# A conv and SwiGLU layer on one core: norm factors by Pool alone, ten of them through scratch, and another order at the end

## The chip, the cores and the metric

The kernel runs on one core of a Trainium2 chip. The core has five engines with instruction queues of their own, each worked off in order: TensorE (PE) multiplies matrices, VectorE (DVE), ScalarE (ACT) and GpSimd (POOL) work on tiles elementwise, SyncE (SP) issues DMAs. ACT issues DMAs too. The metric is the device time of one execution in microseconds (us).

## The reference, cut to what is computed

One layer runs over 2048 tokens of 1024 features in f32. The vector c gives six vectors (shift, scale and gate of two halves of the layer). The first half is a gated causal convolution of three taps, the second a SwiGLU FFN with 2816 hidden features. Each half has an RMS norm ahead of it and another behind it: four norms, each of which needs one factor per token.

```python
def rms_norm(x, g):
    xf = x.astype(jnp.float32)
    y = xf * lax.rsqrt(jnp.mean(xf * xf, axis=-1, keepdims=True) + RMS_EPS)
    return (y * g.astype(jnp.float32)).astype(x.dtype)
...
        mod = c_act @ ada_w[i] + ada_b[i]
        sh_m, sc_m, g_m, sh_f, sc_f, g_f = jnp.split(mod, N_ADA, axis=-1)
        h = modulate(rms_norm(x, norm_gains[i, 0]), sh_m, sc_m)
        h = short_conv_mixer(h, conv_w_in[j], conv_w[j], conv_w_out[j])
        x = x + g_m[:, None, :] * rms_norm(h, norm_gains[i, 1])
        h = modulate(rms_norm(x, norm_gains[i, 2]), sh_f, sc_f)
        h = swiglu(h, ffn_w_gate_up[i], ffn_w_down[i])
        x = x + g_f[:, None, :] * rms_norm(h, norm_gains[i, 3])
```

## The kernel before

**Tiles.** Features lie on the 128 partitions, tokens along the free axis. A tile is mostly 128x512: 128 features of one chunk of 512 tokens (CH). The 2048 tokens are two halves `u` = 0, 1, each of two chunks `tok` = 0, 1; 1024 features are 8 tiles (KD).

**Phases and slots.** The four matrix products of the layer (in, out, gu for gate and up, down) run once for each half, in the order in0, out0, in1, out1, gu0, down0, gu1, down1 (L864). Each is done with seven products P1 to P7 in place of eight, on sums of operands (A11, A12, A22, S1 to S4). Each operand is split into an upper and a lower part (names with h and l), so that a 128x128 by 128x512 product is three matmuls. A slot is four such products, twelve matmuls. A loop goes through the slots in order; weights are called up several slots ahead (`supply`: WHOLE 5, BLOCKS 9, SUMS 7, HIGH 5, LOW 4).

**Order.** Every operation goes through one helper (L78) that keeps it in the order in which it is written, on each engine; so all rows of the profile have line 78, and one goes by the names of tiles. The work beside the products is put between them by hand: `later(slots, f)` (L110) runs f so many slots on, and a generator that yields n goes on n slots later. A delay is a place in the order of the program, not a time.

**A norm factor.** Squares (ACT) are added up over feature tiles (POOL, for a part DVE), in a tile 128x512 such as `out0q`. `norm_of_sums` (L254) sums over the partitions on PE: four matmuls with `mean` as the moving operand leave the means of the squares as a 128x4 tile (token t*128 + p at partition p, column t); then `root` (L218) takes the power -0.5:

```python
        G.tensor_tensor(p, v, mhalf, ALU.pow)
        yield 1
        V.tensor_tensor(t, p, p, ALU.mult)
        V.tensor_tensor(t, t, v, ALU.mult)
        V.scalar_tensor_tensor(q, t, -3.0, p, ALU.add, ALU.mult)
```

The three DVE operations are a Newton step that gives -2 times the factor; so the gains in `vt` are scaled by -0.5 at the start (L158). As tokens lie along the free axis, the factor is then needed as a row, the same on all partitions: `diagonal` (L236) puts the 128x4 tile into four diagonal blocks (4 DVE operations), `spread` (L242) multiplies them by a matrix of ones (one f32 matmul, 128x512, into a PSUM bank) and ACT copies that to `rb`, of which there are two (NRB).

**Names.** r0 to r3 are the factors of the input norms, n00 to n11 (half, chunk) those of the norm behind out (`after_out`, L936), m00 to m11 those of the norm ahead of gu (spread as h00 to h11, L1381), o00, o01, o10 those of the norm behind down (`after_down`, L969), last that of the last chunk (`last_half`, L1011). A letter behind the name tells the step: s sums, v with EPS, p power, t and q the Newton step, d diagonal, b the spread in PSUM, r the copy.

**The end.** Behind the last matmul of down1, `last_half` sums the squares of the last chunk (`down1q`, seven tiles, and `lastq`, the eighth), makes the factor, spreads it (`lastb`), multiplies the eight tiles `down1z` with it on DVE and adds x: for tiles 4, 5, 6, 7, 0 (ON_PE) on PE, into PSUM banks `lastx` that hold x, with an ACT copy and a DMA of ACT behind; for tiles 1, 2, 3 on DVE, with a DMA of SP.

**The start.** `start` (L1076) computes c's vectors with DVE and PE (`ada`, `pms`, `mB`) and the first chunk's factor r0, while x and the first weights land. Matmuls on a constant tile (`warm`, L1203; tile `w`) keep PE busy meanwhile.

Of the kernel before, what the change touches and what calls it, by code (L numbers as in the profile page):

```python
# [10 lines left out]
F32 = mybir.dt.float32  # L11
# [38 lines left out]
def hybrid_conv_layer(  # L50
# [107 lines left out]
    V.tensor_scalar(vt[:, VG : VG + 4 * KD], vt[:, VG : VG + 4 * KD], -0.5, None, ALU.mult)  # L158
# [59 lines left out]
    def root(v, name):  # L218

        p, t = small(4, name + "p"), small(4, name + "t")  # L220
        G.tensor_tensor(p, v, mhalf, ALU.pow)
        yield 1
        q = sb.tile([P, 4], F32, tag="q", bufs=8, name=name + "q")
        V.tensor_tensor(t, p, p, ALU.mult)
        V.tensor_tensor(t, t, v, ALU.mult)
        V.scalar_tensor_tensor(q, t, -3.0, p, ALU.add, ALU.mult)
        return q
# [21 lines left out]
    def spread_later(q, name, put, lag=4):  # L249
        dg = diagonal(q, name)  # L250
        yield lag
        put(spread(dg, name))

# [260 lines left out]
    class Group:  # L514
# [134 lines left out]
        def ready_z(self, c):  # L649
            ph = self.ph  # L650
            tok, n = {"11": (0, self.i), "12": (0, self.i + 4), "21": (1, self.i), "22": (1, self.i + 4)}[c]
            z = ph.z(tok, n)
            if c == "12":
                A.copy(z, self.pa)
            ph.tiles_done[tok] += 1
            scaled_z = partial(A.activation, z, z, AF.Copy, scale=col(mG[1], n))
            if ph.last and ph.tiles_done[1] == KD:
                ph.sq = tmp("lastq")
                A.activation(ph.sq[:, :CH], z, AF.Square)
                scaled_z()  # L660
            else:
                add_square(ph.acc, tok, z, f"{ph.name}q{tok}{n}", V if ph.last and c == "21" else G, 0.5 if ph.last else 1)
                if ph.last and tok:
                    later(1, scaled_z)
            ph.tile_ready(tok, n, z)
            if ph.tiles_done[tok] == KD:
                ph.half_ready(tok)

    def add_square(acc, key, z, name, E=G, lag=1):
        if key not in acc:  # L670
            acc[key] = tmp(name)
            A.activation(acc[key][:, :CH], z, AF.Square)
        else:
            sq = tmp(name)
            A.activation(sq[:, :CH], z, AF.Square)
# [260 lines left out]
    def after_out(ph, tok):  # L936
# [5 lines left out]
        yield (24 if u == 0 else 34) + 8 * tok  # L942
        yield from spread_later(q, f"n{u}{tok}", partial(put, rb, 0))
# [23 lines left out]
        rb1[u, tok] = yield from norm_of_sums(acc[0], f"m{u}{tok}")  # L967

    def after_down(ph, tok):  # L969
# [8 lines left out]
        if not ph.last:  # L978
            yield 22 + 10 * tok
        yield from spread_later(q, f"o{u}{tok}", partial(put, rb, 0), 2 if ph.last else 4)  # L980
# [28 lines left out]
    ON_PE = (4, 5, 6, 7, 0)  # L1009

    def last_half(ph):  # L1011
# [8 lines left out]
        st = bank("lasts")  # L1020
        for k in ON_PE[:2]:
            add_x(k)
        for i, sq in enumerate((ph.acc[tok], ph.sq)):
            for t in range(4):
                PE.matmul(col(st, 4 * i + t), sq[:, t * P : (t + 1) * P], mean, start=True, stop=True)
        for k in ON_PE[2:]:
            add_x(k)
        v = small(4, "lastv")
        V.tensor_scalar(v, st[:, :4], EPS, None, ALU.add)
        V.tensor_tensor(v, v, st[:, 4:8], ALU.add)  # L1030
        dg = diagonal(at_once(root(v, "last")), "last")
        b = bank("lastb")
        PE.matmul(b, one, dg[:, :CH], start=True, stop=True)
        for k in ON_PE + tuple(k for k in range(KD) if k not in ON_PE):
# [6 lines left out]
            else:  # L1041
                V.tensor_tensor(xt, xt, z, ALU.add)
# [315 lines left out]
    for ph in phases[1:]:  # L1358
# [18 lines left out]
        else:  # L1377
            rb = {}
            src = lambda t, tok, kk, u=ph.u: SP.dma_start(t, x1_d[u][tok][:, kk * 4 : kk * 4 + 4, :])
            for tok, op in ((0, "P1"), (1, "P7")):  # L1380
                go = lambda u=ph.u, tok=tok, rb=rb: run(spread_later(rb1[u, tok], f"h{u}{tok}", partial(put, rb, tok)))  # L1381
                at(op, -14 - 2 * ph.u, go)
# [101 lines left out]
```

## Time and profile before

| | us |
|---|---|
| median of 3 runs | 1967.44 (1966.73 to 1967.9) |
| the profiled execution | 1968.11 |
| its span | 1966.3 |
| PE busy in the span | 1939.7 |
| DMA moved | 459.51 MB, mean 234 GB/s |
| granted PE clock, mean | 0.999 |

The span runs from the first to the last instruction of the trace; the profiled execution's own time is 1.8 us longer. Starts in the timeline count from the beginning of the span. "Busy" counts an engine's own operations, and matmuls are pipelined, so that two in a row overlap in the rows. A row of the timeline gives start, duration, engine, operation, out<-in, shape and, in brackets, the idle time of the engine ahead of it and who ended it.

The last matmul of down1 ends at 1946.5 us. The slices of the page show PE at nine tenths or more in all but the first and the last:

```profile
PE   8899999999999999999999999999999999999998
DMA  9369979769996764677665987477554342386534
```

### The profile page before, as it was taken

The page shows a single profiled execution, that of the slowest core. Times are in us where ns is not written, and L with a number is a line of the kernel's source. Part 1 is how long each engine was busy: PE and PEld are TensorE (multiplying, and loading weights), DVE is VectorE, ACT ScalarE, POOL GpSimd, SP SyncE. Part 2 cuts the span into 40 slices and gives each one's busy share as a digit, 9 for nine tenths or more (in the row PEclk, how much of TensorE's full clock was granted, in tenths as well). Part 3 has the DMA queues.
Part 4 walks back from the last instruction along what each step waited for, and adds up shares of the span by engine and source line. Part 5 has one row for each costly group of instructions (what it writes and reads, how often), then busy time and mean ns, then how long its engine had stood idle before and what let it go on. Part 6 is the DMA issues. An engine that isn't in the chain of part 4 may idle for free.

```text
span 1966.3 us, 24998 instructions
## 1 busy us (share of the span) xinstructions
PE 1939.7 (99%) x8468; PEld 1572.9 (80%) x8468; DVE 1463.6 (74%) x2159; ACT 870.3 (44%) x1430; POOL 343.1 (17%) x224
## 2 busy tenths in 40 slices
PE   8899999999999999999999999999999999999998
PEld 4578887878888888888888888888888888888886
DVE  5998898978998876997776765586776655665466
ACT  4633457534336643443333454463333333444452
POOL 0012112311221301244331310120100100111010
PEclk9999999999999999999999999999999999999999
DMA  9369979769996764677665987477554342386534
GB/s 389 137 230 378 332 248 352 267 214 362 324 315 236 263 222 148 223 241 248 208 216 186 304 297 261 183 278 267 199 192 135 125 142 97 118 316 229 197 132 133
DMA packets 204752, 459.51 MB, mean 234 GB/s; under 512 B 22864, under 2 KB 38352, under 8 KB 198224
## 3 DMA queue, kind: packets, MB, share of 16 engines
q1 hardware_dynamic: 180000, 403.52, 59.4%
q10 hardware_dynamic: 24624, 54.40, 7.2%
q8 instruction: 66, 1.08, 0.2%
q14 instruction: 62, 0.51, 0.1%
HBM read 326.75 MB, written 131.07 MB: 233 GB/s over the span
## 4 chain that ended last, share of the span: by engine, by line
PE 92%; DVE 3%; issue 2%; DMA 2%; ACT 1%; POOL 0%; ACTq 0%; POOLq 0%; SPq 0%; DVEq 0%
PE gu0P L78 21%; PE gu1P L78 21%; PE in0P L78 11%; PE down0P L78 11%; PE in1P L78 10%; PE down1P L78 9%; PE out1P L78 4%; PE out0P L78 3%; DMA x<-xx 0%; DMA in0a<-xt_d 0%; DMA c<-c_row_d 0%; PE pms L78 0%; DVE down1z L78 0%; DVE in1y L78 0%; DMA in7P2k<-kin7P 0%
## 5 line engine op out<-in xcount | busy, mean ns | idle before, releaser
L78 DVE TENSOR_TENSOR gu1a<-gu1P,gu1a 128x512 f32<-128x512 f32 x63 | 43.5, 691 | 108.7 <-PE gu1P L78 108.7
L78 DVE TENSOR_TENSOR gu0a<-gu0P,gu0a 128x512 f32<-128x512 f32 x63 | 43.3, 688 | 69.5 <-PE gu0P L78 67.7
L78 POOL TENSOR_TENSOR gu1a<-gu1a 128x512 f32<-128x512 f32 x11 | 19.0, 1726 | 363.5 <-DVE gu1g11s L78 42.5
L78 ACT COPY gu1a<-gu1P 128x512 f32<-128x512 f32 x42 | 24.7, 588 | 98.5 <-PE gu1P L78 87.4
L78 POOL TENSOR_TENSOR nq<-nq,nq 128x512 f32<-128x512 f32 x28 | 41.4, 1477 | 133.8 <-ACT nq L78 129.0
L78 ACT COPY gu0a<-gu0P 128x512 f32<-128x512 f32 x42 | 24.5, 588 | 84.3 <-PE gu0P L78 81.5
L78 DVE CUSTOM_DVE_ANT_0 ada<-ada,c 128x512 f32<-128x512 f32 x80 | 60.1, 761 | 0.0
L78 ACT COPY gu1g<-gu1P 128x512 f32<-128x512 f32 x24 | 14.1, 589 | 92.9 <-PE gu1P L78 92.9
L78 POOL TENSOR_TENSOR down0q<-down0q,down0q 128x512 f32<-128x512 f32 x14 | 23.9, 1706 | 144.1 <-ACT down0q L78 144.0
L78 POOL TENSOR_TENSOR gu0a<-gu0a 128x512 f32<-128x512 f32 x11 | 18.2, 1658 | 170.5 <-ACT gu0a L78 47.5
L78 ACT COPY gu0g<-gu0P 128x512 f32<-128x512 f32 x24 | 14.1, 589 | 75.9 <-PE gu0P L78 75.4
L78 POOL TENSOR_TENSOR down1q<-down1q,down1q 128x512 f32<-128x512 f32 x10 | 16.1, 1615 | 148.6 <-ACT down1q L78 148.5
L78 DVE TENSOR_TENSOR gu1g<-gu1P,gu1g 128x512 f32<-128x512 f32 x24 | 16.6, 691 | 27.4 <-ACT gu1g L78 26.0
L78 DVE TENSOR_TENSOR down2P<-down2P,down2P 128x512 fp32r<-128x512 f32 x14 | 12.0, 854 | 28.6 <-ACT down2P L78 28.6
L78 ACT ACTIVATE gu1a<-gu1a 128x512 f32<-128x512 f32 x42 | 26.6, 633 | 13.2 <-DVE xo L78 6.0
L78 ACT ACTIVATE gu0a<-gu0a 128x512 f32<-128x512 f32 x42 | 26.6, 632 | 11.5 <-DVE gu0a L78 10.2
L78 POOL TENSOR_TENSOR out1q<-out1q,out1q 128x512 f32<-128x512 f32 x14 | 22.3, 1594 | 51.3 <-ACT out1q L78 51.2
L78 POOL TENSOR_TENSOR out0q<-out0q,out0q 128x512 f32<-128x512 f32 x14 | 22.5, 1606 | 45.1 <-ACT out0q L78 44.9
L78 DVE TENSOR_TENSOR xx<-xx,zz 128x512 f32<-128x512 f32 x32 | 28.2, 880 | 1.1
L78 DVE TENSOR_TENSOR gu0g<-gu0P,gu0g 128x512 f32<-128x512 f32 x24 | 16.5, 689 | 14.7 <-ACT gu0g L78 13.3
L78 ACT ACTIVATE nq<-xx 128x512 f32<-128x512 f32 x32 | 20.2, 631 | 15.9 <-DVE xx L78 15.9
L78 DVE TENSOR_TENSOR down10P<-down10P,down10P 128x384 fp32r<-128x384 f32 x14 | 8.6, 615 | 22.0 <-ACT down10P L78 22.0
(3225 smaller groups left out, 6728.5 us busy)
## 6 DMA issues: line engine op xcount, KB each, us to landing
ada<-ada_d SPq DMA_DIRECT2D x64, 256.0 KB, 5.2
act0A<-gu0a SPq DMA_DIRECT2D x33, 256.0 KB, 3.5
act1A<-gu1a SPq DMA_DIRECT2D x33, 256.0 KB, 2.7
ada<-ada_d SPq DMA_DIRECT2D x16, 512.0 KB, 9.4
zz<-z SPq DMA_DIRECT2D x32, 256.0 KB, 5.5
xx<-xt_d SPq DMA_DIRECT2D x32, 256.0 KB, 5.4
x<-xx ACTq DMA_DIRECT2D x32, 256.0 KB, 5.5
down0S<-act0S SPq DMA_DIRECT2D x8, 1024.0 KB, 7.1
```

The lines of the kernel that those rows point to most:

```text
L78: return tc.keep_in_program_order(f(*args, **kwargs))
```

## The change

It has four parts.

1. `root` takes POOL's power as the factor. The three DVE operations behind it go in all norms, and the scaling of `vt` at the start with them (the factor is no longer -2 times itself).
2. Ten factors (n00, n01, n10, n11, those of m, and o00, o01) are no longer spread by a diagonal, PE and ACT. `keep_row` has ACT write the 128x4 tile, 16 bytes from each partition, into a row of 2 KB in DRAM eight slots after the factor is there; `repeat_later` has SP load that row to all 128 partitions (256 KB) eight slots ahead of its use. The point of use stays where it was. r0 to r3, o10 and last are spread as before.
3. So that 16 bytes of a partition are four tokens in a row, token p*4+t must end at partition p, column t. For that the 80 squares of the ten norms are written with their tokens in another order: ACT reads a tile in order and writes with a step of 128 elements (512 bytes). The squares of down1 stay as they are.
4. The end: the sums of the seven tiles of `down1q` stand on PE some slots ahead of the last products; the EPS is added to them; the diagonal and its spread go in four pieces, one after the other; two matmuls `lastw` fill PE behind them; tiles 4 to 7 are added on PE (and go out by ACT), 1 and 2 on POOL, 0 and 3 on DVE (and go out by SP), in the order 0, 4, 1, 5, 6, 2, 7, 3.

```diff
-    V.tensor_scalar(vt[:, VG : VG + 4 * KD], vt[:, VG : VG + 4 * KD], -0.5, None, ALU.mult)
...
     def root(v, name):
-        p, t = small(4, name + "p"), small(4, name + "t")
-        G.tensor_tensor(p, v, mhalf, ALU.pow)
+        q = sb.tile([P, 4], F32, tag="q", bufs=8, name=name + "q")
+        G.tensor_tensor(q, v, mhalf, ALU.pow)
         yield 1
-        q = sb.tile([P, 4], F32, tag="q", bufs=8, name=name + "q")
-        V.tensor_tensor(t, p, p, ALU.mult)
-        V.tensor_tensor(t, t, v, ALU.mult)
-        V.scalar_tensor_tensor(q, t, -3.0, p, ALU.add, ALU.mult)
         return q
...
+    def keep_row(q, name):
+        row = scratch([CH], name + "w")
+        later(8, lambda: A.dma_start(row.rearrange("(p t) -> p t", t=4), q))
+        return row
+
+    def repeat_later(row, name, put):
+        rb = sb.tile([P, CH], F32, tag="rb", bufs=NRB, name=name + "r")
+        SP.dma_start(rb, row.rearrange("(a n) -> a n", a=1).to_broadcast((P, CH)))
+        yield 8
+        put(rb)
...
-                add_square(ph.acc, tok, z, f"{ph.name}q{tok}{n}", V if ph.last and c == "21" else G, 0.5 if ph.last else 1)
+                add_square(ph.acc, tok, z, f"{ph.name}q{tok}{n}", V if ph.last and c == "21" else G, 0.5 if ph.last else 1, not ph.last)
                 if ph.last and tok:
                     later(1, scaled_z)
+                    if ph.tiles_done[1] == KD - 1:
+                        later(1.5, partial(all_but_one, ph))
...
-    def add_square(acc, key, z, name, E=G, lag=1):
+    def add_square(acc, key, z, name, E=G, lag=1, in_turn=True):
+        def square(t):
+            if in_turn:
+                A.activation(t[:, :CH].rearrange("p (t n) -> p n t", t=4), z.rearrange("p (n t) -> p n t", t=4), AF.Square)
+            else:
+                A.activation(t[:, :CH], z, AF.Square)
...
         q = yield from norm_of_sums(ph.acc[tok], f"n{u}{tok}")
-        yield (24 if u == 0 else 34) + 8 * tok
-        yield from spread_later(q, f"n{u}{tok}", partial(put, rb, 0))
+        row = keep_row(q, f"n{u}{tok}")
+        yield (20 if u == 0 else 30) + 8 * tok
+        yield from repeat_later(row, f"n{u}{tok}", partial(put, rb, 0))
...
-        rb1[u, tok] = yield from norm_of_sums(acc[0], f"m{u}{tok}")
+        q = yield from norm_of_sums(acc[0], f"m{u}{tok}")
+        rb1[u, tok] = keep_row(q, f"m{u}{tok}")
...
         q = yield from norm_of_sums(ph.acc[tok], f"o{u}{tok}")
-        if not ph.last:
-            yield 22 + 10 * tok
-        yield from spread_later(q, f"o{u}{tok}", partial(put, rb, 0), 2 if ph.last else 4)
+        if ph.last:
+            yield from spread_later(q, f"o{u}{tok}", partial(put, rb, 0), 2)
+        else:
+            row = keep_row(q, f"o{u}{tok}")
+            yield 18 + 10 * tok
+            yield from repeat_later(row, f"o{u}{tok}", partial(put, rb, 0))
...
-    ON_PE = (4, 5, 6, 7, 0)
+    ON_PE, ON_POOL, LAST_TURN = (4, 5, 6, 7), (1, 2), (0, 4, 1, 5, 6, 2, 7, 3)
+
+    def sums_of_squares(ph, sq, first):
+        for t in range(4):
+            PE.matmul(col(ph.st, t + 4 * first), sq[:, t * P : (t + 1) * P], mean, start=True, stop=True)
+
+    def all_but_one(ph):
+        ph.st = bank("lasts")
+        sums_of_squares(ph, ph.acc[1], True)
...
-        st = bank("lasts")
+        v = small(4, "lastv")
+        V.tensor_scalar(v, ph.st[:, 4:8], EPS, None, ALU.add)
         for k in ON_PE[:2]:
             add_x(k)
-        for i, sq in enumerate((ph.acc[tok], ph.sq)):
-            for t in range(4):
-                PE.matmul(col(st, 4 * i + t), sq[:, t * P : (t + 1) * P], mean, start=True, stop=True)
+        sums_of_squares(ph, ph.sq, False)
         for k in ON_PE[2:]:
             add_x(k)
-        v = small(4, "lastv")
-        V.tensor_scalar(v, st[:, :4], EPS, None, ALU.add)
-        V.tensor_tensor(v, v, st[:, 4:8], ALU.add)
-        dg = diagonal(at_once(root(v, "last")), "last")
-        b = bank("lastb")
-        PE.matmul(b, one, dg[:, :CH], start=True, stop=True)
-        for k in ON_PE + tuple(k for k in range(KD) if k not in ON_PE):
+        V.tensor_tensor(v, v, ph.st[:, :4], ALU.add)
+        q = at_once(root(v, "last"))
+        dg = tmp("lastd")
+        b, warm = bank("lastb"), bank("lastw")
+        for t in range(4):
+            c = slice(t * P, (t + 1) * P)
+            V.tensor_scalar(dg[:, c], ident, q[:, t : t + 1], None, ALU.mult)
+            PE.matmul(b[:, c], one, dg[:, c], start=True, stop=True)
+        for _ in range(2):
+            PE.matmul(warm, one, dg[:, :CH], start=True, stop=True)
+        for k in LAST_TURN:
...
-                V.tensor_tensor(xt, xt, z, ALU.add)
+                (G if k in ON_POOL else V).tensor_tensor(xt, xt, z, ALU.add)
...
-                go = lambda u=ph.u, tok=tok, rb=rb: run(spread_later(rb1[u, tok], f"h{u}{tok}", partial(put, rb, tok)))
-                at(op, -14 - 2 * ph.u, go)
+                go = lambda u=ph.u, tok=tok, rb=rb: run(repeat_later(rb1[u, tok], f"h{u}{tok}", partial(put, rb, tok)))
+                at(op, -18 - 2 * ph.u, go)
```

How this moves instructions, at three places of the program. First, PE's queue in gu1, where o00's factor is spread (`gu1P` are the PSUM banks of the products, behind the comma stands the operand that is loaded as weights). Before, and then of the change:

```order
L78 MATMUL gu1P_0_11326<-gu1S2h,gu0P6k 128x512 x2
L78 MATMUL gu1P_0_11326<-gu1S2l,gu0P6k 128x512
L78 MATMUL o00b<-o00d,one 128x512
L78 MATMUL gu1P_1_11347<-gu1S2h,gu1P6k 128x512 x2
L78 MATMUL gu1P_1_11347<-gu1S2l,gu1P6k 128x512
```
```order
L78 MATMUL gu1P_0_11222<-gu1S2h,gu0P6k 128x512 x2
L78 MATMUL gu1P_0_11222<-gu1S2l,gu0P6k 128x512
L78 MATMUL gu1P_1_11243<-gu1S2h,gu1P6k 128x512 x2
L78 MATMUL gu1P_1_11243<-gu1S2l,gu1P6k 128x512
L78 MATMUL gu1P_1_11243<-gu1S2h,gu1P6k 128x512 x2
```

The spread stood between two products and is gone; so it is at the nine other places. Second, ACT's queue in in1 where n00's factor is written, of the change (casts make the upper parts of operands, copies empty PSUM), and SP's queue where it is read (`gu0b` and `in6P` are weights, `kgu0P` and `y1A` stores):

```order
L78 ACTIVATE in1d<-in1d,mB_95 128x512 x4
L78 CAST in1S2h<-in1a 128x512 x4
L78 CAST in1S1h<-in1c 128x2048
L78 DMA n00w<-n00q 128x4
L78 CAST in1S4h<-in1b 128x2048
L78 COPY in1c_21_3431<-in1P_0_3230 128x512
```
```order
L78 DMA kgu0P_3595<-gu0P_3575 128x1024
L78 DMA kgu0P_3603<-gu0P_3597 128x1024
L78 DMA n00r<-n00w 128x512
L78 DMA in6P1k<-kin6P_1208 128x1024
L78 DMA y1A_106<-in1y_3552 128x512
```

Both DMAs are new and stand between rows that were neighbours before. Third, the end of PE's queue, before and then of the change (`down1P` is the last bank of the products, `xl` holds x):

```order
L78 MATMUL down1P_3_15723<-down1A_15793,down11P_16059 128x512
L78 MATMUL lastx_16146<-xl_15911,ident 128x512
L78 MATMUL lastx_16148<-xl_15913,ident 128x512
L78 MATMUL lasts<-mean,down1q_15853 128x1 x4
L78 MATMUL lasts<-mean,lastq 128x1 x4
L78 MATMUL lastx_16158<-xl_15915,ident 128x512
L78 MATMUL lastx_16160<-xl_15917,ident 128x512
L78 MATMUL lastx_16162<-xl_15903,ident 128x512
L78 MATMUL lastb<-lastd,one 128x512
L78 MATMUL lastx_16146<-down1z_15378,ident 128x512
```
```order
L78 MATMUL down1P_3_15602<-down1A_15667,down11P_15933 128x512
L78 MATMUL lastx_16026<-xl_15785,ident 128x512
L78 MATMUL lastx_16028<-xl_15787,ident 128x512
L78 MATMUL lasts<-mean,lastq 128x1 x4
L78 MATMUL lastx_16034<-xl_15789,ident 128x512
L78 MATMUL lastx_16036<-xl_15791,ident 128x512
L78 MATMUL lastb<-lastd,one 128x128 x4
L78 MATMUL lastw<-lastd,one 128x512 x2
L78 MATMUL lastx_16026<-down1z_15257,ident 128x512
```

The four sums of `down1q` are gone from here; they now stand 21 matmuls of `down1P` earlier, behind the products with `down3P`. The spread is four matmuls.

More of the change, by code (lines that the diff above doesn't have):

```diff
@@ L667, in ready_z @@
                 ph.half_ready(tok)
-    def add_square(acc, key, z, name, E=G, lag=1):
+    def add_square(acc, key, z, name, E=G, lag=1, in_turn=True):
[4 more added lines that the diff above has]
+                A.activation(t[:, :CH], z, AF.Square)
         if key not in acc:
             acc[key] = tmp(name)
-            A.activation(acc[key][:, :CH], z, AF.Square)
+            square(acc[key])
         else:
             sq = tmp(name)
-            A.activation(sq[:, :CH], z, AF.Square)
+            square(sq)
             later(lag, lambda: E.tensor_tensor(acc[key][:, :CH], acc[key][:, :CH], sq[:, :CH], ALU.add))
```

## The prediction

> **What bounds the kernel now.** I read the page first, then the windows, then the waits of TensorE (PE), because the share of busy time alone doesn't say where PE is the limit.
>
> ```profile
> span 1966.3 us, 24998 instructions
> PE 1939.7 (99%) x8468; PEld 1572.9 (80%) x8468; DVE 1463.6 (74%) x2159; ACT 870.3 (44%) x1430; POOL 343.1 (17%) x224
> 0.00:480.00 480.00, 461.43 (x1947) 356.02 (x1948) 402.13 (x687) 234.40 (x404) 78.91 (x53) 1.00 0.80 288
> 440.00:480.00 40.00, 39.60 (x173) 32.15 (x172) 33.27 (x52) 17.21 (x32) 4.31 (x4) 1.00 1.01 349
> 480.00:1945.00 1465.00, 1465.00 (x6480) 1210.18 (x6479) 1052.11 (x1452) 631.61 (x1020) 263.13 (x170) 1.00 0.63 218
> ```
>
> The last three rows are windows: length, then busy time of PE, its weight loads, DVE, ACT and POOL, the granted clock, the DMA share and GB/s. From 480 to 1945 us PE is busy for all 1465.00 us at full clock. There the time is the sum of what PE executes, and nothing else; only PE instructions that go away shorten it. Before 480 us PE is idle for 18.6 us in sum, so there waits count too. The table of PE's waits names them:
>
> ```profile
> PE in1P L78 <- ACT in1c L78: 2.3, 2, 1.4
> PE out0P L78 <- ACT out0z L78: 1.7, 1, 1.7
> PE r1b L78 <- DVE r1d L78: 0.6, 1, 0.6
> ```
>
> Columns: who waits for whom, us in all, times, longest. After 1946 us comes a serial tail. So the change falls into four pieces: PE's stream, the early waits, the start and the tail.
>
> **1. Ten spreads leave PE's stream.** In the chain of waits each is one piece (start, us, what), from the first to the tenth (n00b, n01b, h00b, h01b, n10b, n11b, h10b, h11b, o00b, o01b); one of them stands in the timeline below it:
>
> ```profile
> 442.19 0.86 PE n00b L78 x2
> ...
> 1435.14 0.86 PE o01b L78 x2
> ```
> ```profile
> 1341.62 1.02 PE L78 MATMUL o00b<-o00d,one 128*128 128x512 f32 x2
> 1342.08 1.03 PE L78 MATMUL gu1P<-gu1S2h,gu1P6k 128*128 128x512 f32 x2
> ```
>
> An f32 product is two passes. 10 x 0.86 = **-8.6 us**. The four diagonals of each on DVE and the PSUM copy on ACT go too; in the window from 480 on these engines are busy 72% and 43%, so that is worth nothing by itself. The least that I allow is eight spreads, -6.9, if the two at 442 and 487 us only give their time to a wait for DMAs.
>
> In their place ACT issues ten writes of 2 KB (128 pieces of 16 bytes), SP ten broadcasts of 256 KB. The nearest row for the broadcast is the same form, one row to 128 partitions:
>
> ```profile
> c<-c_row_d SPq DMA_DIRECT2D x8, 256.0 KB, 5.4
> x<-xx ACTq DMA_DIRECT2D x32, 256.0 KB, 5.5
> ```
>
> (last number: median us from issue to landing.) The broadcast is issued eight slots ahead of its use, a slot being 12 matmuls of about 0.227 us, 2.72 us: 21.8 us against 5.4. From write to read there are at least ten slots, 27 us. No trace of before has a 16-byte write; between 0 (hidden) and 5.5 us (the 256 KB store) it fits either way. Ten broadcasts are 2.6 MB on top of 459.51 MB, 0.6%. Only up to 480 us are the transfers themselves near their limit (share 0.80, 1.01 at 440 to 480); there two broadcasts may push weight loads back. I take **+0.3** (0 to +0.8).
>
> **2. The waits before 480 us.** At 316 us PE waits 1.71 us for a chain that the timeline shows:
>
> ```profile
> 307.26 2.33 POOL L78 TENSOR_TENSOR out0q<-out0q,out0q 128x512 f32<-128x512 f32 x1 [2.79 <-ACT out0q L78]
> 308.36 1.25 DVE L78 TENSOR_TENSOR r3t<-r3p 128x4 f32<-128x4 f32 x1
> 309.93 0.68 DVE L78 TENSOR_TENSOR out0z<-out0P,out0z 128x512 f32<-128x512 f32 x1
> 313.66 0.63 ACT L78 ACTIVATE out0q<-out0z 128x512 f32<-128x512 f32 x1 [1.87 <-DVE out0z L78]
> 315.23 0.58 ACT L78 COPY out0z<-out0P 128x512 f32<-128x512 f32 x1
> 315.86 0.73 PE L78 MATMUL out0P<-out0S10h,out0P 128*128 128x512 f32 x2 [1.71 <-ACT out0z L78]
> ```
>
> The correction r3t, r3t, r3q holds DVE from 308.36 to 309.93, 1.57 us, of which 1.25 is one 128x4 product that stands still beside POOL's add. Without it out0z comes 1.57 earlier, then the square, and with it ACT's queue. The square, however, is now written in steps of 128 elements. POOL's add follows its squares and may also collide with DVE's r3d instead. I take half, **-0.7** (-1.6 to +1.0, see rival B).
>
> At 396 us the same correction lies ahead of a longer chain:
>
> ```profile
> 373.87 1.25 DVE L78 TENSOR_TENSOR n00t<-n00p 128x4 f32<-128x4 f32 x1
> 375.43 2.49 DVE L78 TENSOR_TENSOR in1S3l<-in1e,in1S3h 128x512 fp32r<-128x512 f32 x4
> 394.18 1.91 ACT L78 CAST in1S4h<-in1b 128x2048 fp32r<-128x2048 f32 x1 [5.05 <-DVE in1b L78]
> 396.62 0.73 PE L78 MATMUL in1P<-in1S1h,in3P5k 128*128 128x512 f32 x2 [0.84 <-ACT in1c L78]
> ```
>
> DVE is then busy up to in1b; 1.56 us less ahead of it is more than PE's wait: **-0.8**, no more than 0.84, and 0 if ACT's squares eat it. The other in1c wait (1.4) hangs on a weight's DMA and stays. At r1b the three DVE products before r1d go (about 0.2 us apart, as in the tail below), 0.5 of a wait of 0.6: **-0.5**. Together **-2.0** (-2.9 to +0.5; beyond that lies only rival B).
>
> **3. The start.** The change also takes away the scaling of vt:
>
> ```profile
> 5.21 0.18 DVE L78 TENSOR_SCALAR vt<-vt 128x32 f32<-128x32 f32 x1 [4.17 <-DMA vt<-vec_d]
> 5.99 8.52 PE L78 MATMUL wb<-w,one 128*128 128x512 f32 x16 [5.99 <-DVE w L78]
> 14.69 1.13 PE L78 MATMUL r0b<-r0d,one 128*128 128x512 f32 x2 [0.18 <-DVE r0d L78]
> 15.74 3.61 PE L78 MATMUL pms<-ada,cact 128*1 128x256 f32 x16
> ```
>
> The memset of w followed it in DVE's queue; now it runs at about 1 us, and the warming matmuls at 1.6 to 10. PE would then stand idle for some 4 us ahead of r0b, at 14.1. What such a gap does, this trace shows at 79 to 87 us, where PE was only half busy:
>
> ```profile
> 82.50:83.00 0.50, 0.09 (x1) 0.00 (x0) 0.50 (x2) 0.32 (x1) 0.00 (x0) 1.00 0.00 0
> 83.00:83.50 0.50, 0.07 (x1) 0.07 (x1) 0.50 (x2) 0.00 (x0) 0.00 (x0) 1.00 0.00 0
> 84.00:85.00 1.00, 1.00 (x4) 0.75 (x3) 1.00 (x2) 0.00 (x0) 0.00 (x0) 0.50 0.00 0
> ```
>
> Some 3.4 us at clock 0.50 follow. At 14 us that would make r0b 1.72 instead of 0.86 and some of the sixteen pms twice as long (0.22 each more), against 0.6 us of earlier r0 and about 0.35 us of slack to the vector mB: **+0.5** (0 to +1.2, **rival D**). The Trainium skill, "TensorE: Matmul & The Clock Gate", part 1 on the HAM clock gate, says that an idle window of about 3.4 us lets the clock fall to half, and that the window runs freely. The row at 84 us (0.50) agrees; by that rule a gap of 4 us may or may not hold a whole window, and the sum is +0.5 either way.
>
> **4. The tail.**
>
> ```profile
> 1941.04 0.68 DVE L78 TENSOR_TENSOR down1q<-down1q,down1q 128x512 f32<-128x512 f32 x1
> 1948.04 0.95 PE L78 MATMUL lasts<-mean,down1q 128*128 128x1 f32 x8
> 1951.41 0.16 DVE L78 TENSOR_TENSOR lastt<-lastp 128x4 f32<-128x4 f32 x1 [1.13 <-POOL lastp L78]
> 1952.00 0.87 DVE L78 TENSOR_SCALAR lastd<-ident,lastq 128x128 f32<-128x128 f32 x4
> 1952.93 1.12 PE L78 MATMUL lastb<-lastd,one 128*128 128x512 f32 x2 [0.36 <-DVE lastd L78]
> 1954.09 3.68 DVE L78 TENSOR_TENSOR down1z<-down1z,lastb 128x512 f32<-128x512 f32 x6 [1.22 <-PE lastb L78]
> 1958.53 2.98 SPq L78 DMA_DIRECT2D out_d<-xl  x3
> L78 POOL TENSOR_TENSOR down1q<-down1q,down1q 128x512 f32<-128x512 f32 x10 | 16.1, 1615 | 148.6 <-ACT down1q L78 148.5
> ```
>
> (The last row is a group of the page: count, sum, mean ns of one.) Step by step: of the eight sums, the four of down1q go ahead of the last products. That saves their 0.8 behind them (0.95 with an overlap) and the EPS add of 0.2: -1.0. But PE's stream, full until then, gets the 0.8, and PE comes there at about 1941.4 while DVE's add ends at 1941.72, 0.3 more: +1.1. The correction goes: 1951.41 to 1952.00, -0.6. The diagonal and its spread take 2.09 us (1952.00 to 1954.09) and in four pieces overlap: the last diagonal ends at +0.87, a quarter spread and the hand-over some 0.56: -0.66. From the first product with lastb to the last issue there were about 7.1 us (to SP's third). Now two adds are POOL's (1.6 us each), SP has tiles 0 to 3 and ACT tiles 4 to 7; eight products and two adds of DVE, with about 0.6 us between starts, and a hand-over give 6.9: -0.2. Sum **-1.4** (-2.2 to -0.4; the upper end where POOL's adds hold DVE as at 308 us).
>
> **Sum.** -8.6 + 0.3 - 2.0 + 0.5 - 1.4 = **-11.2 us**. The profiled execution took 1968.1 (span 1966.3 and 1.8 around it): **1956.9 us**. The median of the runs shown, 1967.44, lies 0.7 lower, which the range includes.
>
> **Rivals.**
>
> *B, the stepped writes are dear.* Eighty ACT squares write one element in every 512 bytes. No row shows this. ACT has room (43%), but two squares lie on the chain to 316 us and some on that to 396. ACT's nearest longer square is this group:
>
> ```profile
> L78 ACT ACTIVATE xr<-xr 128x1024 f32<-128x1024 f32 x8 | 8.4, 1052 | 6.1 <-DMA xr<-x_d 6.0
> ```
>
> 0.42 us more for each (1.05 against the 0.63 quoted) eats the gain at 316 and 396; 1.28 more (as long as the 1.91 of the 128x2048 cast) turns them into +1.0 and +2.5. Time: between 1958.4 and **1961.9**. The Trainium skill, "SBUF — State Buffer", on the port swizzle (Door 1), says in a note that every access that crosses into another 16-byte line pays a penalty, with no price; here every element would, so by it this rival holds and the time would be that of B. No row of before can confirm it. 0.25.
>
> *C, the removed matmuls are only partly gain.* If weights set the pace up to 490 us, n00b and n01b become waits: -6.9 in place of -8.6, **1958.6**. For it: the DMA share of 1.01 there; against: PE is busy for 39.60 of those 40 us. 0.12.
>
> *S, slower: SP stands behind the row writes.* SP issues in order; each of the ten broadcasts must wait until its row is written, and the rotating DMA semaphores make the eighth transfer after each write wait for its landing as well. A write has ten slots (27 us) until SP comes to its broadcast, and the weights queued behind that are called five slots (13.6 us) ahead. So from about 41 us between a write's place in the program and its landing (its turn on ACT behind a cast such as that at 394 us, and its 128 small pieces) PE waits for all beyond. At 42.4 us in each of the ten places the loss, 15 us, is 3.9 more than the gain; at 43 us the time is 1956.9 + 10 x 2.1 = **1978**. That is eight times the 5.5 of the store quoted, and nothing in the trace points to it. 0.03.
>
> *N, the change doesn't do what it says*, since the engines keep program order: the pieces at the end don't overlap and the sums stall PE for longer (tail 0 in place of -1.4): **1958.3**. 0.1. D by itself gives **1957.6**; 0.1.
>
> My forecast, within 1.5 us of 1956.9, has 0.4. All but S lie between 1954 and 1962; the bounds of the terms added up alone give 1953.5 (with the lower median) and 1962. **Range 1953.5 to 1962.0.** A measurement tells about 0.2%, 3.9 us, from no change. Faster by more needs under 1963.5: 0.92; within it, where B, C and N come together or S begins, 0.05; slower 0.03.
>
> **What will show it.** The ten tiles with names in b gone from PE, and PE's waits between 480 and 1945 still none; a wait there for ACT or DMA speaks for S. The mean of the squares on ACT against 0.63 us, and PE's waits at about 315 and 395 us (B). The clock and the length of pms at 14 to 19 us (D). The landing of the row writes and broadcasts, and PE's waits at 430 to 480 us (C). In the tail, DVE's first product with lastb about 2.5 us after POOL's pow starts (3.7 before), and the last issue 6.9 us behind it. The prediction is wrong if the stream from 480 to 1435 us shrinks by less than nine times 0.86, or if the early waits grow.

## The result, and the profile after

| | before | changed |
|---|---|---|
| median of 6 runs each, us | 1968.07 | 1961.12 (1959.04 to 1961.87) |
| ratio to before (95% interval) | | 0.9967 (0.9956 to 0.9977) |
| profiled execution, us | 1968.11 | 1961.33 |
| its span, us | 1966.3 | 1959.5 |

The ratios are over executions with a mean clock of 0.993 or more; one execution of the run e3_no_spreads below, at a mean clock of 0.556, took 3271.96 us and is not in its ratio.

The kernel is faster by 0.33%, 6.5 us (0.23 to 0.44% by the interval; the two profiled executions lie 6.8 us apart), where 11.2 were forecast. The time lies in the range, near its upper end. The page of the changed kernel:

```profile
span 1959.5 us, 24903 instructions
...
PE 1934.8 (99%) x8454; PEld 1570.0 (80%) x8454; DVE 1446.5 (74%) x2069; ACT 899.6 (46%) x1419; POOL 343.8 (18%) x226
```

PE's sum fell by 4.9 us only, although ten spreads of 0.86 are gone: some operations at the start are longer (shown below), and lastw is new at the end. ACT's sum rose by 29 us, although ten copies are gone. The groups of ACT say why (count, sum, mean ns of one):

```profile
L78 ACT ACTIVATE nq<-xx 128x512 f32<-128x512 f32 x32 | 37.1, 1159 | 17.0 <-DVE xx L78 17.0
...
L78 ACT ACTIVATE out0q<-out0z 128x512 f32<-128x512 f32 x16 | 18.2, 1154 | 12.5 <-DVE out0z L78 12.3
...
L78 ACT ACTIVATE down1q<-down1z 128x512 f32<-128x512 f32 x15 | 9.5, 633 | 22.2 <-DVE down1z L78 16.3 <-DMA out_d<-xo 5.8
```

The same square takes 1154 to 1159 ns with the stepped output and 633 without (down1q was not changed): 0.52 us for each of eighty. PE's waits, whole span (who waits for whom, us, times, longest), and a window of the stretch in which PE had no idle time before:

```profile
PE r0b L78 <- DVE r0d L78: 2.3, 1, 2.3
...
PE in1P L78 <- ACT in1c L78: 2.0, 2, 1.1
...
PE in1P L78 <- ACT in1C L78: 1.7, 2, 1.4
...
PE out0P L78 <- ACT out0z L78: 1.4, 1, 1.4
PE gu0P L78 <- ACT gu0a L78: 1.3, 2, 0.7
```
```profile
480.00:1945.00 1465.00, 1462.27 (x6481) 1209.04 (x6480) 1039.09 (x1389) 652.67 (x1011) 263.73 (x171) 1.00 0.64 219
```

Of those 1465 us, 2.7 are idle now. What the stretches lost or gained is read from the starts of the same product in both traces, before and then changed:

```profile
22.22 0.73 PE L78 MATMUL in0P<-in0A11h,in0P 128*128 128x512 f32 x2 [0.22 <-ACT in0A11h L78]
...
481.69 0.62 PE L78 MATMUL in1P<-in1S4h,in1P 128*128 128x512 f32 x2
...
1436.30 0.39 PE L78 MATMUL gu1P<-gu1S3l,gu6P 128*128 128x512 f32 x1
```
```profile
22.94 0.73 PE L78 MATMUL in0P<-in0A11h,in0P 128*128 128x512 f32 x2
...
479.69 0.62 PE L78 MATMUL in1P<-in1S4h,in1P 128*128 128x512 f32 x2
...
1430.07 0.39 PE L78 MATMUL gu1P<-gu1S3l,gu6P 128*128 128x512 f32 x1
```

The change is 0.7 us late at the first product, 2.0 early at the second and 6.2 early at the third. So from the second to the third it gains 4.2 us, where nine spreads (9 x 0.86 = 7.7) left the stream. The 3.5 that are missing are the idle 2.7 and a longer first matmul or two behind each wait.

In the timeline there are three new waits behind 480 us, all for ACT; the fourth row is the early one at 396 us, which was 0.84 and is 0.85:

```profile
395.46 0.73 PE L78 MATMUL in1P<-in1S1h,in3P5k 128*128 128x512 f32 x2 [0.85 <-ACT in1c L78]
...
562.06 0.74 PE L78 MATMUL in1P<-in1S2h,in10P 128*128 128x512 f32 x2 [1.38 <-ACT in1C L78]
...
709.28 0.74 PE L78 MATMUL gu0P<-gu0S1h,gu0P5k 128*128 128x512 f32 x2 [0.68 <-ACT gu0a L78]
...
890.80 0.73 PE L78 MATMUL gu0P<-gu0S2h,gu11P 128*128 128x512 f32 x2 [0.61 <-ACT gu0a L78]
```

The start, as timeline and windows (length, busy time of PE, its loads, DVE, ACT, POOL, granted clock, DMA):

```profile
1.64 10.16 PE L78 MATMUL wb<-w,one 128*128 128x512 f32 x16 [1.64 <-DVE w L78]
...
14.08 1.62 PE L78 MATMUL r0b<-r0d,one 128*128 128x512 f32 x2 [2.29 <-DVE r0d L78]
...
15.63 4.77 PE L78 MATMUL pms<-ada,cact 128*1 128x256 f32 x16
...
21.23 0.16 DVE L78 TENSOR_TENSOR mB<-pms,vt 128x2 f32<-128x2 f32 x1 [0.68 <-PE pms L78]
```
```profile
14.00:15.00 1.00, 0.92 (x2) 0.30 (x2) 1.00 (x4) 0.00 (x0) 0.00 (x0) 0.79 1.06 438
15.00:16.00 1.00, 1.00 (x2) 0.09 (x2) 1.00 (x5) 0.27 (x1) 0.00 (x0) 0.50 1.08 455
...
17.00:18.00 1.00, 1.00 (x4) 0.26 (x2) 0.00 (x0) 0.00 (x0) 0.00 (x0) 0.50 0.95 375
18.00:19.00 1.00, 1.00 (x6) 0.40 (x5) 0.81 (x2) 0.26 (x1) 0.00 (x0) 1.00 1.06 408
```

PE stands idle for 2.29 us, then, from some 14.6 us on, runs at clock 0.50 up to 18 us; mB, which the first features wait for, comes at 21.23 where it came at 20.51 before (the timeline's row of the same addition). And the tail:

```profile
1941.09 0.40 PE L78 MATMUL down1P<-down1A,down11P 128*128 128x512 f32 x1
...
1943.04 1.00 PE L78 MATMUL lasts<-mean,lastq 128*128 128x1 f32 x8
...
1944.32 1.02 POOL L78 TENSOR_TENSOR lastq<-lastv,mhalf 128x4 f32<-128x4 f32 x1 [29.24 <-DVE lastv L78]
...
1946.91 0.69 DVE L78 TENSOR_TENSOR down1z<-down1z,lastb 128x512 f32<-128x512 f32 x1 [0.66 <-PE lastb L78]
...
1953.94 0.34 ACTq L78 DMA_DIRECT2D out_d<-xl  x1
```

From POOL's power to the first product with lastb it is 2.59 us (3.73 before), from there to the last issue 7.0 (7.1 before).

### The profile page after: what moved, and what is told of

It is laid out like the page before. It is cut to its first block, busy times and chain, and to the rows that moved or that the text cites. A ratio compares the mean times of both kernels' runs of the same rounds, so it can differ in the third digit from the quotient of the medians.

```text
span 1959.5 us, 24903 instructions
## 1 busy us (share of the span) xinstructions
PE 1934.8 (99%) x8454; PEld 1570.0 (80%) x8454; DVE 1446.5 (74%) x2069; ACT 899.6 (46%) x1419; POOL 343.8 (18%) x226
## 4 chain that ended last, share of the span: by engine, by line
PE 80%; DVE 8%; DMA 6%; ACT 3%; issue 2%; SPq 0%; ACTq 0%; POOL 0%; DVEq 0%
PE gu1P L78 21%; PE gu0P L78 18%; PE in0P L78 11%; PE down0P L78 11%; PE down1P L78 11%; PE in1P L78 3%; PE out1P L78 2%; PE out0P L78 2%; DMA x<-xx 1%; PE pms L78 1%; DMA kgu1P<-gu1P 1%; DVE in1b L78 0%; DVE in1y L78 0%; DVE gu0a L78 0%; DMA xr<-x_d 0%
## 5 line engine op out<-in xcount | busy, mean ns | idle before, releaser
L78 ACT ACTIVATE nq<-xx 128x512 f32<-128x512 f32 x32 | 37.1, 1159 | 17.0 <-DVE xx L78 17.0
L78 DVE TENSOR_TENSOR down2P<-down2P,down2P 128x512 fp32r<-128x512 f32 x14 | 11.2, 801 | 29.0 <-ACT down2P L78 29.0
L78 ACT ACTIVATE down0q<-down0z 128x512 f32<-128x512 f32 x16 | 18.4, 1153 | 14.9 <-DVE down0z L78 14.8
```

The source lines that it names most:

```text
L78: return tc.keep_in_program_order(f(*args, **kwargs))
```

## The experiments

Two theories at first. **A**: the dear squares hold ACT's queue, and PE waits for it. **B**: PE, freed of the spreads, runs into chains beside it that didn't become shorter. All runs, each against runs of the kernel before on the same chip; the last column is PE's idle time behind 480 us, summed from its waits:

| run | ratio (95%) | span, us | PE waits |
|---|---|---|---|
| change | 0.9967 (0.9956 to 0.9977) | 1959.5 | 2.7 |
| e1_plain_squares | 0.9950 (0.9935 to 0.9965) | 1955.5 | 0.6 |
| e2_step_in_sums | 0.9983 (0.9973 to 0.9993) | 1962.8 | none |
| e3_no_spreads | 0.9961 (0.9947 to 0.9975) | 1958.9 | 1.9 |
| e4_step_squares_only | 0.9999 (0.9990 to 1.0009) | 1965.4 | none |
| e5_row_4byte | 1.0018 (1.0008 to 1.0028) | 1973.8 | 9.7 |
| e6_row_4byte_warm10 | 1.0028 (1.0018 to 1.0038) | 1971.4 | 7.9 |
| e7_no_spreads_no_newton | 0.9944 (0.9931 to 0.9957) | 1954.7 | none |
| e8_no_newton_only | 0.9989 (0.9980 to 0.9998) | 1965.4 | none |
| e9_step_read | 1.0040 (1.0027 to 1.0052) | 1977.0 | 13.7 |
| e10_step_read_warm10 | 1.0034 (1.0021 to 1.0046) | 1973.2 | 12.8 |
| e11_old_end | 1.0039 (1.0025 to 1.0052) | 1976.6 | 12.4 |
| e12_e7_step_squares | 0.9948 (0.9934 to 0.9961) | 1956.3 | 0.7 |

A profiled execution lies up to 2.5 us off its kernel's median (in e5 4.6), so the intervals decide on sizes and the waits on places.

**e1_plain_squares**: the change, but the squares in order.

```diff
-                add_square(ph.acc, tok, z, ..., 0.5 if ph.last else 1, not ph.last)
+                add_square(ph.acc, tok, z, ..., 0.5 if ph.last else 1, False)
...
-    def add_square(acc, key, z, name, E=G, lag=1, in_turn=True):
+    def add_square(acc, key, z, name, E=G, lag=1, in_turn=False):
```

> The changed kernel with the eighty squares written in order (plain 128x512), all else as in the change; the ten rows then hold their tokens in another order, so the factors reach other tokens. In the changed kernel a square takes 1154 to 1159 ns on ACT against 631 before, and PE has new waits for ACT that before had not: 1.38 us at 562, 0.68 at 709, 0.61 at 891, and the waits at 316 (1.4) and 396 (0.85) hardly shrank. Theory A (the dear squares hold ACT's queue, and PE waits for it): the squares fall back to 0.63 us, the waits at 562, 709 and 891 go, those at 316 and 396 shrink by about 1 and 0.8, and the time falls by 3 to 4.5 us against the changed kernel (to about 1957). Theory B (PE, freed of the spreads, runs into chains beside it that didn't become shorter: transfers, their shared semaphores, DVE): the three new waits stay and only 316 and 396 shrink, 1 to 2 us less.

A group of ACT, and the row of PE's waits for the one at 316 us:

```profile
L78 ACT ACTIVATE nq<-xx 128x512 f32<-128x512 f32 x32 | 20.2, 631 | 16.2 <-DVE xx L78 16.2
```
```profile
PE out0P L78 <- ACT out0z L78: 0.9, 1, 0.9
```

The square is back at 631 ns, the three waits are gone (one of 0.6 for in1c is new), and the wait at 316 us fell to 0.9. The span is 4.0 us shorter; by the ratios 0.17%, 3.3 us. The intervals of the two ratios overlap a little, so the size is less sure than the waits, which are gone. Theory A holds as to the changed kernel: the dear squares are the cause. The way from them to each wait wasn't followed; ahead of that at 562 us, for one, ACT's queue had stood 4.41 us for DVE's in10b, not for a square.

**e4_step_squares_only**: the kernel before with the stepped squares alone (`square(t)` of the change, nothing else).

> The kernel before with only the eighty squares written in steps of 128 elements (their factors then stand at other tokens). Squares of 1.15 us. Theory A: PE's waits at 316 (1.7) and 396 (0.84) grow by 0.5 to 1 us each and a new one appears near 562: slower by 1.5 to 3 us than the kernel before. Theory B: the two early waits grow, but none is new behind 480 us: slower by 0.5 to 1.5 us.

Neither theory had this right: the squares took 1155 ns and the kernel before lost nothing (0.9999, an interval of some 2 us to each side), no wait is new, and the one at 316 us is even 1.2 instead of 1.7. So the dear squares have no price of their own; it depends on how early PE is.

**e3_no_spreads**: the kernel before without the ten spreads.

```diff
     def spread_later(q, name, put, lag=4):
+        if name in ("n00", "n01", "n10", "n11", "h00", "h01", "h10", "h11", "o00", "o01"):
+            yield lag
+            rb = sb.tile([P, CH], F32, tag="rb", bufs=NRB, name=name + "r")
+            G.memset(rb, 1.0)
+            put(rb)
+            return
```

> The kernel before with the ten spreads left out and nothing in their place: the factors in rb are a constant 1.0 that POOL writes (diagonals, f32 matmuls and PSUM copies of these ten gone, Newton steps and plain squares kept). No new transfer, no dear square. Theory A: the full 10 x 0.86 = 8.6 us comes off the kernel before, no new wait of PE behind 480 us. Theory B: new waits of PE behind 480 us show up here too, at about 562, 709 and 891 (some 2.7 us in sum), and the gain is 5 to 7 us. If n00b and n01b only gave their time to a wait for transfers (440 to 490 us), the gain is 6.9.

PE's waits from 480 us on:

```profile
PE out1P L78 <- DVE out3P L78: 0.7, 1, 0.7
PE in1P L78 <- ACT in1C L78: 0.5, 1, 0.5
PE gu0P L78 <- ACT gu0a L78: 0.5, 1, 0.5
PE in1P L78 <- DVE in9P L78: 0.2, 1, 0.2
```

The second and third are those at 562 and 709 us, at smaller size, with plain squares and without any new transfer; the span is 7.4 us shorter, not 8.6. So theory B holds too: these chains stood right behind PE.

**e7_no_spreads_no_newton**: e3, and the power as the factor in all norms (the start is left as before).

```diff
+        G.tensor_tensor(q, v, mhalf, ALU.pow)
         yield 1
-        V.tensor_tensor(t, p, p, ALU.mult)
-        V.tensor_tensor(t, t, v, ALU.mult)
-        V.scalar_tensor_tensor(q, t, -3.0, p, ALU.add, ALU.mult)
```

> The run without the ten spreads (kernel before, factors of these ten a constant 1.0, plain squares), and in addition without the three DVE operations of the Newton step in all norms; the scaling at the start stays, so the start is as before and the factors of the remaining norms are off by -2. Without the spreads PE still waited 0.47 at 562, 0.46 at 709, 0.65 at 619 and 0.23 at 544. Theory B1 (DVE's short chains ahead of these are the second holder): those at 562 and 709 go, and 316 and 396 shrink by 0.5 to 1 each; 2 to 3 us less than the run without spreads. Theory B2 (they hang on transfers or on ACT): they stay, only 316 and 396 shrink.

All four waits are gone and the one at 316 us is 0.6; the span is 4.2 us below e3's and 11.6 below that of before. Three DVE operations of a 128x4 tile were the second holder (B1). This is what the two removals give together where nothing is put in their place.

**e12_e7_step_squares**: e7 with the stepped squares.

> The run without spreads and without Newton step (kernel before, factors of these ten a constant, span 1954.7), and in addition the eighty squares in steps of 128 elements. No new transfers. In the kernel before, the stepped squares alone cost nothing (ratio 0.9999). Theory A2 (they cost because PE is earlier there, and ACT's queue has no room left): 3 to 4.5 us more than without them, new waits of PE for ACT at 562, 709 or 891. Theory T (they cost only together with the twenty transfers that share ACT's and SP's queues): 0 to 1 us more and no new wait behind 480 us.

It lies between the two theories: 1.6 us more than e7 in the span (0.8 by the ratios, whose intervals overlap), with the wait at 709 us back,

```profile
PE gu0P L78 <- ACT gu0a L78: 0.7, 1, 0.7
```

and 316 us at 1.4 in place of 0.6, but none at 562 or 891. So the wait at 709 comes from the squares as soon as PE is early. With the Newton step gone, those at 562 and 891 came only where the new transfers were too (e3 has 0.5 at 562 without them, but with the Newton step): in the changed kernel they stand behind the writes of m00's and m10's rows, which ACT issues at 545.55 and 885.68 us.

**e5_row_4byte**: e1 with the tokens put in order by the row write.

```diff
-        later(8, lambda: A.dma_start(row.rearrange("(p t) -> p t", t=4), q))
+        later(8, lambda: A.dma_start(row.rearrange("(t p) -> p t", t=4), q))
```

> The plain squares made right in another place: ACT writes the row of factors in 4-byte pieces (token t*128+p from partition p, column t), 512 pieces in place of 128 of 16 bytes; the rest is the change, and the result is that of the reference. The row has 27 us until SP reads it; the row write of the changed kernel is the nearest. If the pieces stay hidden: the time of the run with plain squares (span 1955.5, about 3 to 4 us under the changed kernel), no waits of PE for ACT at 562, 709 and 891. If the small pieces hold the transfers' engines or their shared semaphores: new waits of PE or ACT for a DMA near the ten writes, 0.5 us or more each, and no gain over the changed kernel.

The pieces are not hidden: PE's timeline has three long waits, each 11 to 30 us behind a row write (n01, m00 and m10, issued at 401.9, 547.1 and 891.6):

```profile
432.04 0.74 PE L78 MATMUL in1P<-in1S1h,in0P 128*128 128x512 f32 x2 [3.19 <-ACT in1c L78]
...
560.02 0.79 PE L78 MATMUL in1P<-in1A12h,in10P 128*128 128x512 f32 x1 [4.05 <-DVE in10P L78]
...
902.98 1.22 PE L78 MATMUL gu0P<-gu0S2h,gu11P 128*128 128x512 f32 x2 [5.14 <-ACT gu0a L78]
```

This is near to rival S's mechanism (the transfers behind a slow row write come late), at the places of the waits at 562 and 891 us of the changed kernel, at three to eight times the size. Behind m00's write SP's queue has a weight's store (kgu2P), then six issues and then a load of `ada`. From the store to that load it took 5.6 us in e1 (545.57 to 551.15) and 10.6 in e5 (549.10 to 559.73), and ACT's next cast waits for the DMA of kgu2P:

```profile
559.33 0.62 ACT L78 CAST gu2P<-gu2b 128x512 fp32r<-128x512 f32 x1 [10.26 <-DMA kgu2P<-gu2P]
```

Such a wait costs more than its length, because the clock is at half behind it, here from 559 us to nearly 570:

```profile
562.00:563.00 1.00, 1.00 (x4) 0.81 (x3) 1.00 (x3) 0.00 (x0) 0.00 (x0) 0.50 1.06 383
```

Ahead of the wait e5 is 2.1 us behind e1 at the same product (553.44 us in e1, 555.58 in e5); at the end of the half clock it is 10.7 behind (558.45 and 569.14). The wait of 4.05 us has cost some 8.5.

**e2_step_in_sums**: e1 with the order made by PE's weight loads.

```diff
+                PE.matmul(st[:, t : t + 1], acc[:, t:CH:4] if in_turn else acc[:, t * P : (t + 1) * P], mean, ...)
```

> As the run with plain squares, but the order of tokens is made in the sums instead: PE loads every fourth column of the summed squares as weights (a step of 16 bytes) in the forty 128x1 sums of the ten norms, so that token p*4+t stands at partition p again and the result is that of the reference. If a weight load with that step costs no more than a plain one, the time is that of the run with plain squares; if each of the 40 (80 passes) costs 0.1 us more, 8 us more would be lost, and the time would be above the changed kernel's.

The tile view of the first such norm gives for its eight loads (ns: least, median, most)

```profile
L78 PEld LDWEIGHTS n00s<-mean,out0q x8: 308/329/332, 354.7 to 356.4; 128*128 128x128 f32 x8
```

where the changed kernel has 192. The matmuls follow each other 0.12 us later; 80 of them are 9.8 us in PE's full stream, and the span is 7.3 above e1's. No wait stands behind 480 us: PE, later again, has its cover back.

**e9_step_read**: e1 with the order made where DVE reads the factor.

```diff
+        put(rb[:, :].rearrange("p (n t) -> p t n", t=4))
...
+            V.scalar_tensor_tensor(four(z), four(z), col(mG[0], k), rb[0], ALU.mult, ALU.mult)
```

> Plain squares again, 16-byte pieces as in the change, and the order of tokens made where the factor is used: the row stands permuted in rb, and the 96 DVE products that use the ten factors read it in steps of 16 bytes (four tokens), so the result is that of the reference. In the run with plain squares such a product takes about 0.74 us. If a read in such steps is as fast as a plain one, the time is that of the run with plain squares (span 1955.5). If it costs as much as the stepped write of ACT (0.52 us each), DVE gets 50 us more and PE waits at 316 to 709 as in the changed kernel or longer: 1960 or more.

The eight products of one norm, in e9 and then in e1 (ns: least, median, most; one of the eight is far longer in both):

```profile
L78 DVE SCALAR_TENSOR_TENSOR zz<-zz,mG,n01r x8: 1122/1136/2184, 504.4 to 547.7; 128x512 f32<-128x512 f32 x8
```
```profile
L78 DVE SCALAR_TENSOR_TENSOR zz<-zz,mG,n01r x8: 741/746/1782, 500.9 to 541.1; 128x512 f32<-128x512 f32 x8
```

Each takes 0.39 us more. PE waits 13.7 us in all behind 480. Of the engines beside PE, DVE had the least room (74% busy before).

**e6_row_4byte_warm10** and **e10_step_read_warm10**: e5 and e9 with `warm(10)` in place of `warm(8)`.

> As the run with 4-byte rows, and ten warming matmuls at the start in place of eight (4 more passes of 0.43 us), so that PE is idle some 0.6 us ahead of r0b in place of 2.3. Theory D (the gap lets the clock fall): clock 1.00 at 14 to 18 us where the changed kernel has 0.50, r0b some 1.1 us and the sixteen pms 3.6 in place of 4.8, mB 0.7 earlier (20.5), time 0.5 to 0.8 less than the run with 4-byte rows. Otherwise (the clock falls by its own period, or the products wait for their data): pms as long as in the changed kernel and no difference.

> As the run with stepped reads, with ten warming matmuls in place of eight. In the runs with 4-byte rows this moved mB from 21.3 to 20.4 us. Expected: 0.7 to 0.9 us less than the run with stepped reads (span about 1954.7), clock 1.00 at 14 to 18 us.

e10 at the start:

```profile
14.05 1.12 PE L78 MATMUL r0b<-r0d,one 128*128 128x512 f32 x2 [1.05 <-DVE r0d L78]
...
15.11 3.61 PE L78 MATMUL pms<-ada,cact 128*1 128x256 f32 x16
...
20.46 0.16 DVE L78 TENSOR_TENSOR mB<-pms,vt 128x2 f32<-128x2 f32 x1
```
```profile
15.00:16.00 1.00, 1.00 (x6) 0.37 (x6) 1.00 (x5) 0.59 (x1) 0.00 (x0) 1.00 1.01 426
```

With a gap of 1.05 us the clock stays at 1.00, the sixteen pms take 3.61 us again and mB is 0.7 us earlier than in e9 (21.15, where pms took 4.04). e5 and e6 don't show this: mB stands at 21.3 and 20.4, but in e5 the clock was 1.00 from 14 to 19 us and pms took 3.62, although PE had been idle for 3.83 us; r0's factor came later there. So the length of the gap alone doesn't decide. At the end of the runs such a part of a microsecond is below what the ratios tell (e6 isn't faster than e5 by them).

**e8_no_newton_only**: the kernel before with the first part of the change alone.

> The kernel before with the first part of the change alone: POOL's power is the factor, the Newton step and the scaling at the start gone. Expected by the terms of the prediction: start +0.7 (clock 0.50 at 14 to 18 us, as the changed kernel showed), r1b -0.4, wait at 316 0.5 to 1.5 less, wait at 396 0.8 less, end -0.6: in sum -1.6 to -2.6. If the early chains are held by something else than the Newton step, 316 and 396 stay within 0.3 of before and the sum is -0.3.

By the ratio 0.11%, 2.2 us, as the terms said. The wait at 316 us is 0.6 (from 1.7), those for in1c 1.9 in sum (from 2.3), r1b 0.2 (from 0.6). The span (1965.4) shows less, since in that one execution the clock was 0.50 up to 20 us: the sixteen pms took 5.48 us and mB stands at 22.71.

**e11_old_end**: e10 with the end of the kernel before (but no Newton step).

> As the run with stepped reads and ten warming matmuls, but with the end of the kernel before (eight sums behind the last product, one diagonal and spread, tiles 4, 5, 6, 7, 0 on PE and 1, 2, 3 on DVE); the Newton step stays away. By the traces of before and after, the new end without the Newton step's 0.6 is worth: sums -1.0 and +1.2, spread in pieces -0.56, last issue -0.1, landing of the last piece +0.45, in sum 0.0. By the prediction it was worth -0.8. So: within 0.3 us of the run with the new end by the first, 0.8 us more by the second; PE reaches lastx 1.2 us earlier and lastb about 0.5 later in either case.

From the start of o10b to the end of the span it is 61.2 us in e10 (1912.02 to 1973.19) and 61.0 in e11 (1915.62 to 1976.59). The new end by itself gives nothing. What the change gains there, 0.5 (61.65 before, 1904.65 to 1966.30, and 61.16 after, 1898.39 to 1959.55), is the Newton step: e8, with the old end and without that step, has 61.1 as well (1904.34 to 1965.4).

## Why the prediction was right, and where it was off

The right column goes by the starts of the same products in the two traces.

| term | predicted | in the traces |
|---|---|---|
| ten spreads | -8.6 | -8.6, and +3.5 lost at new waits behind 480 us |
| transfers | +0.3 | no sum of their own; part of the waits at 562 and 891 |
| waits before 480 us | -2.0 | -1.9, in part at other places |
| start | +0.5 | +0.7 |
| tail | -1.4 | -0.5 |
| sum | -11.2 | -6.8 (span: -6.8) |

**The direction and the main term** were right: the spreads were most of the gain, and where each had stood the stream is 0.7 to 0.9 us shorter. But the prediction's own sign of being wrong came up too: from 480 to 1435 us the stream should shrink by nine times 0.86, 7.7, and it shrank by 4.2. That the time still fell into the range is in part luck, since the range was wide enough for rivals that weren't what happened.

**The step that failed** is in point 2, with rival B. I set the stepped squares against two early waits, at half the gain, and saw no place for them behind 480 us, because PE had no wait there. The runs show that such a stretch is not a stretch without rivals: chains of ACT, DVE and transfers stood close behind PE (e3: 1.9 us of waits as soon as the spreads are gone). The change frees PE by a few microseconds and at the same time makes such chains dearer. Its squares cost 0.52 us each, between B's two ends, and 3.3 us (by the ratios, e1) to 4.0 us in all. Rival B's time, 1958.4 to 1961.9, is where the kernel came out, but by B's own sum, which knows only the waits at 316 and 396, squares dearer by 0.52 give some 1959 (an estimate, by a straight line between its two ends). The rest came from behind 480 us, so B's number fits better than its account. The Trainium skill, "SBUF — State Buffer", Door 1, said that each access to another 16-byte line pays; the 1154 ns against 631 agree.

**The waits before 480 us** gave nearly the forecast sum, -1.9, but by luck: at 316 us the wait shrank by 0.3 in place of 0.7, at 396 not at all in place of 0.8, for the same reason. r1b gave 0.4 of the 0.5. The rest came from places that the prediction left out or took as fixed: the wait at 432 us, which was to stay, went from 1.4 to 1.1, and there are small gains elsewhere, less a new wait of 0.3 for in1C. With plain squares and no Newton step the wait at 316 falls to 0.6 (e7, e8): the cause was the one named.

**The start**: rival D's mechanism held, at 0.7 of its 0 to 1.2, and e10 undoes it with two more warming matmuls. The gap was 2.29 us in place of some 4, since the warming matmuls took 10.16 us. (The stretch at 79 to 84 us from which the prediction took the effect was not half busy, but busy for 3.23 of its 5 us.) The size of the loss is not firm: mB stands at 20.5 to 21.3 us in the traces with the old start and at 21.1 to 22.7 in those with the new one and eight warming matmuls.

**The tail** gave 0.5 of 1.4. The sums, the Newton step and the first product came as reckoned (2.59 us for 2.5). What was off: the landing behind the last issue, 5.6 us (1953.94 to 1959.5) where it had been some 5.1, and the pieces of the spread, 0.56 for 0.66. e11 and e8 say that the rebuilt end without the Newton step is worth nothing.

**Rival S** was priced far too low in one respect: it needed no lateness of 41 us. In e5 writes of small pieces made PE wait 3 to 5 us each at three places; n01's write lands after 11.8 us where the changed kernel has 5.1, m00's after 9.7 where it has 4.9, and the broadcasts that read them land as before (6.4 and 7.0 us, 6.6 and 7.1 in the changed kernel). The transfers behind the write in SP's queue suffer, not the broadcast. **Rivals C and N**: n00b and n01b were not lost to transfers (weights made PE wait 0.4 us up to 480 before and 0.2 after). The pieces at the end did overlap.

**The range.** The bounds of the terms as the prediction gives them add up to -13.7 and -4.8, so to 1953.7 (with the lower median) and 1963.3, not to 1953.5 and 1962; the result lies inside either way.

What stays open: at 562 and 891 us, how much is the row write itself and how much the shared order of transfers behind it. Without the transfers (e12) and with plain squares (e1) the waits are gone, with slower writes (e5) they grow; the semaphores and the transfer engines weren't tried apart. No version with the reference's result was found that beats the change: three other places for the permutation cost more than ACT's (e2, e5, e9). POOL, which had the most room (17% busy), wasn't tried for it. The change with `warm(10)` alone wasn't run either.

## What to carry to other kernels

An engine that is busy without a gap hides how close the others are; before work is taken from it, look for the chains that will end last next, and don't make these dearer in the same edit. The price of an off-path operation is not a constant: the same eighty squares cost nothing that could be measured in one kernel and 3 to 4 us in the other. A change of layout had to be paid for at each of the four places tried here, and least on the engine with the most room of the three engines tried, ACT.

## What the runs showed of the hardware

- An element step in an f32 operand is dear on each engine tried: ACT writing in steps of 512 bytes 1154 ns in place of 631, DVE reading one operand in steps of 16 bytes 1136 in place of 746 (median of 8), PE loading weights in steps of 16 bytes 329 in place of 192.
- PE idle for 2.29 us at the start was enough for some 3.4 us at half clock (14.6 to 18 us); 1.05 us (e10) was not, and neither was 3.83 us (e5). In e5 a wait of 4.05 us in the full stream was followed by about ten us at half clock and cost some 8.5 us in all.
- A wait of PE in a full stream costs more than its idle time: 2.7 us of idle at three waits, 3.5 us of the stream, at full clock.
- A 128x4 row written in 512 pieces of 4 bytes, ten times in a kernel, cost 13 us by the ratios against 128 pieces of 16 bytes (1.0018 and 0.9950; 18 us between the two profiled executions), by the waits of others and the half clock behind them.
